# A decoder layer on one core: start offsets of the split weights, the layout of the KV weights, and elementwise work between GpSimd, VectorE and ScalarE

## Chip, core and metric

The kernel runs on one core of a Trainium2 chip. The metric is the device time of one execution in microseconds, here the median of three runs. The engines are TensorE (PE, with its weight loads PEld), VectorE (DVE), ScalarE (ACT), GpSimd (POOL) and SyncE (SP), which issues the DMAs.

## What is computed

One decoder layer in float32 on 256 tokens of width 2048: a mixer of two attentions, a cross-attention over 256 memory tokens, and an MLP of width 8192 with a squared ReLU, each followed by a layer norm of the scaled residual.

```python
def reference(x, mem, ...):
    h = x
    for l in range(DEPTH):                      # DEPTH = 1
        mix = hybrid_mixer(h, w_in[l], ...)
        h = layer_norm(DN_ALPHA * h + mix, ln1_g[l], ln1_b[l])
        xa = memory_cross_attention(h, mem, xa_w_q[l], xa_w_kv[l], xa_w_o[l])
        h = layer_norm(DN_ALPHA * h + xa, ln2_g[l], ln2_b[l])
        ff = squared_relu_mlp(h, mlp_w1[l], mlp_w2[l])
        h = layer_norm(DN_ALPHA * h + ff, ln3_g[l], ln3_b[l])
    return h

def hybrid_mixer(x, w_in, ...):
    h = x @ w_in                                # queries, keys, values, gates
    y_a = swa_sink_attention(...)               # sliding window of 128, 16 heads
    y_b = nsa_attention(...)                    # compressed, selected and window branch, 16 heads
    merged = sigmoid(g_a) * (y_a @ w_branch_swa) + sigmoid(g_b) * (y_b @ w_branch_nsa)
    return merged @ w_mix_out
```

## The kernel before

**Numbers.** Every float32 matrix product is made of three TensorE products of rounded parts. A weight chunk and an activation are each split into h, the value rounded to the matmul's 32-bit format, and l, the rest; the product is h·h + h·l + l·h.

**Chunks.** The weights come in chunks of 128 x 1024 float32 (512 KB; the first 16 are 1072 wide). SP loads a chunk into a tile `raw` (five buffers). `emit_splits` splits it: ScalarE casts it to h (line 198) and VectorE subtracts h from it to give l (line 199). h and l each have four buffers of 1152 columns, of which a chunk uses a part that begins at a start offset, `shift`, counted in columns of 4 bytes. `run_chunks` goes through all chunks in the program's order: it issues the loads, splits up to three chunks ahead (fewer for the first six, and one less for the chunks in `evac_first`), and issues the chunk's matmuls; `post` empties the PSUM banks at a block's end. Each engine executes its instructions in the order in which they were issued.

**Blocks.** A block is a run of chunks that fill the same PSUM banks.
- `make_c`, the KV block: 16 chunks with all keys, values and gates of the two attentions. Each makes six 432-column matmuls with the values' weights moving (`mm_x`, lines 231 to 238) and fifteen 256-column matmuls with the keys' weights stationary (`mm_w`, lines 246, 248, 249). `kv_parts` says how the raw columns go into h and l: keys first, the values behind from column 640 on, in three copies on each engine (four in the first chunk).
- `block_b`, 512 output columns with the weights stationary. For each 128 x 128 piece there is a pair: line 318 has h stationary and 512 moving columns (the activation's h and l), line 319 has l stationary and 256 moving columns. It is used for the queries of `w_in`, the keys and queries of the cross-attention, and `mlp_w1` from column 1024 on: 20 blocks of 8 chunks. Its offset goes round from chunk to chunk:

```python
shift=((0, 96, 48)[len(chunks) % 3],) * 2))
```

- `block_w`, the first 1024 columns of `mlp_w1`, with the weights stationary, 256 moving columns and the fixed offset (16, 112).
- `block_x`, the rest, with the weights moving in 512 columns and the offset 0; `mlp_w2` is the longest.

**Work beside the chunks.** `Side` holds jobs that run a piece at a time between chunks: the softmaxes (`softmax_job`), transposes and layer norms. In a softmax job VectorE adds the bias and takes the maximum, ScalarE takes the exponentials (line 734), VectorE the reciprocal of the sum, GpSimd multiplies the 512 columns by it (line 745), and TensorE transposes the result (line 749). There are 36 jobs; the 512 columns are two regions of 256 or four of 128. The compressed branch has four such multiplies on GpSimd (line 822). At the end of a `w_branch_nsa` block, `evac_bb` multiplies each PSUM bank by its gate on VectorE (line 955) and GpSimd adds it to `merged` (line 956); those banks are then taken by the next block. A layer norm's `norm_a` is a scale and shift on ScalarE (line 1037), a multiply on VectorE (line 1038) and an add on GpSimd (line 1039). `finish` does the last layer norm behind the row blocks of `mlp_w2` and ends with lines 1044 and 1048 on VectorE and the stores.

Of the kernel before, what the change touches and what calls it, by code (L numbers as in the profile page):

```python
# [12 lines left out]
F32R = mybir.dt.float32r  # L13
# [25 lines left out]
def fp(ap):  # L39
    return ap.bitcast(F32)  # L40


class Chunk:
    def __init__(self, loads, n, mm, pre=None, with_split=None, post=None, cap=AHEAD, extra=None, parts=None, shift=(0, 0)):
        self.loads, self.n, self.mm = loads, n, mm
        self.pre, self.with_split, self.post, self.cap = pre, with_split, post, cap
        self.extra, self.shift = extra, shift
        self.parts = parts or [((lambda r: r[:, :n]),) * 2]

# [61 lines left out]
def layer(ctx: ExitStack, tc: tile.TileContext, x, mem, w_in, attn_sinks, rel_bias_table,  # L111
# [77 lines left out]
    def emit_splits(upto):  # L189
        while state["split"] <= min(upto, len(chunks) - 1):  # L190
            c = state["split"]
            ch = chunks[c]
            if ch.extra:
                h, l = ch.extra()
            else:
                h, l = (split_tile(t)[:, c0:] for t, c0 in zip("hl", ch.shift))
            for src, dst in ch.parts:
                nc.scalar.copy(dst(h), src(raws[c]))  # L198
                nc.vector.tensor_sub(dst(l), src(raws[c]), fp(dst(h)))  # L199
            hs[c], ls[c] = h, l  # L200
            consumed.add(c)
            if ch.with_split:
                ch.with_split()
            state["split"] += 1

    def run_chunks():
        for i, ch in enumerate(chunks):
            if ch.pre:
                ch.pre()
            emit_loads()  # L210
            side.phase("ev")
            ahead = i + min(ch.cap, 1 if i < 3 else 2 if i < 6 else AHEAD)
            emit_splits(min(ahead, i + AHEAD - 1) if i in evac_first else ahead)
            emit_loads()
            ch.mm(hs[i], ls[i])
            if ch.post:
                ch.post()
                emit_splits(ahead)
                emit_loads()
            side.phase("pe")  # L220
# [85 lines left out]
    def block_b(w, n0, rhs, evac, tags=("acc",) * 4, pre=None):  # L306
# [3 lines left out]
        for k0 in range(0, KD, 2):  # L310
# [10 lines left out]
            def post():  # L321
# [4 lines left out]
            chunks.append(Chunk(loads, 1024, mm, pre=pre if k0 == 0 else None, post=post if k0 + 2 == KD else None,  # L326
                                shift=((0, 96, 48)[len(chunks) % 3],) * 2))

# [159 lines left out]
    def kv_loads(k):  # L488
# [8 lines left out]
        return own + more  # L497

    def kv_parts(k):
        def pairs(v0, v1):  # L500
            return (lambda r: r[:, 128:896].rearrange("p (b v n) -> p v b n", v=2, n=P)[:, v0:v1],
                    lambda r: r[:, 128:896].rearrange("p (v b n) -> p v b n", v=2, n=P)[:, v0:v1])

        def cols(c0, c1):
            return (lambda r: r[:, c0:c1],) * 2
        if k == 0:
            return [pairs(1, 2), cols(896, 1072), pairs(0, 1), cols(0, 128)]
        return [pairs(0, 2), cols(896, 1072), cols(0, 128)]

# [61 lines left out]
    def make_c():  # L571
        for k in range(KD):
            def mm(h, l, k=k):
# [4 lines left out]
                xh, xl = xk(k)  # L578
                first, last, V = k == 0, k == KD - 1, slice(640, 1072)
                rows = [slice(s * P, (s + 1) * P) for s in range(2)]  # L580
# [8 lines left out]
                else:  # L589
                    mm_x({(0, 0): a[0][:, :432], (1, 0): a[1][:, :432]},  # L590
                         lambda s: xh[:, rows[s]], lambda s: xl[:, rows[s]], h, l, [(640, 1072)], False, last)
                outs = [a[2][:, :S], cbox["c"][:, :S], cbox["c"][:, S:], a[2][:, S:], a[3][:, :S]]
                mm_w(outs, xh, xl, h, l, first, last, (0, 1, 4), (2, 3, 4), (0, 128, 512, 256, 384))

# [109 lines left out]
    def softmax_job(n, s, qk, regions, order, pv, gate=None, sink=None, first=False, stop=False, done=False, last=False):  # L704
# [36 lines left out]
        if gate is not None:  # L741
            smv = two(sm) if len(gate.shape) == 3 else sm
            nc.vector.tensor_mul(smv, smv, gate)
        pr = p.rearrange("p (r w) -> p r w", r=nr)
        nc.gpsimd.tensor_mul(pr, pr, sm.unsqueeze(2).to_broadcast([P, nr, 512 // nr]))  # L745
        yield "pe"
# [45 lines left out]
    def cmp_job(n):  # L792
# [28 lines left out]
        nc.vector.tensor_mul(cm[:, 1, 0:4], cm[:, 1, 0:4], rowmask.to_broadcast([P, 4]))  # L821
        nc.gpsimd.tensor_mul(pv, pv, cm[:, 1].unsqueeze(2).to_broadcast([P, 8, 32]))
        yield "pe"
# [125 lines left out]
    def evac_bb(n0):  # L949
        def evac(acc):  # L950
            m = merged()
            for (s, b), a in acc.items():
                c = n0 + 512 * b
                t = box["pb"].tile([P, 512], F32, tag="xp", name="gtmp", bufs=3)
                nc.vector.scalar_tensor_tensor(t, box["tb"][:, s, c:c + 512], 1.0, a, op0=OP.add, op1=OP.mult)
                nc.gpsimd.tensor_add(m[:, s, c:c + 512], m[:, s, c:c + 512], t)
            if n0 == 0:
# [75 lines left out]
    def norm_a(s, c0, w, add=None, mul=None):  # L1033
# [4 lines left out]
        (mul or nc.vector).tensor_mul(v, v, gb[:, 0, c0:c0 + w])  # L1038
        (add or nc.gpsimd).tensor_add(v, v, gb[:, 1, c0:c0 + w])

# [90 lines left out]
    def xa_job(h):  # L1131
# [33 lines left out]
        hilo(box["oth"][:, h, :], box["otl"][:, h, :], o[:, :S])  # L1165

    block_b(xa_w_kv[0], 0, me, evac_t("kt", None))
    evac_first.add(len(chunks) - 1)
    block_x(xa_w_kv[0], KD, 512, 256, me, evac_v(0))
# [9 lines left out]
    def after_wo(s, b):  # L1179
# [14 lines left out]
        norm_late(1, 256, 256)  # L1194
        norm_a(0, 256, 256, add=nc.vector)
        norm_shift(1)
# [13 lines left out]
    def between_wo(s, b):  # L1210
        if (s, b) == (1, 2):
            norm_shift(0)
            norm_a(0, 0, 256, mul=nc.gpsimd)

# [147 lines left out]
```

## Time and profile before

| | us |
|---|---|
| median of three runs (lowest, highest) | 1413.92 (1413.91, 1414.34) |
| the profiled execution's own time | 1414.3 |
| its span in the profile | 1412.3 |
| TensorE busy | 1394.8 |
| VectorE busy | 919.2 |
| ScalarE busy | 721.7 |
| GpSimd busy | 113.5 |

The span runs from the first to the last instruction of the profiled execution. A matmul's row has a start and a length; matmuls overlap in the array, so the step from one start to the next tells how long one takes in a row of them. The granted TensorE clock of the execution was 0.997 of full speed.

### The profile page before, as it was taken

Reading aid. Unit: us, or ns where it says so; the run is one execution under the profiler, and the core shown is the slowest. Engines: PE = TensorE matmul, PEld = TensorE weight load, DVE = VectorE, ACT = ScalarE, POOL = GpSimd, SP = SyncE. Lnnn points to the kernel's source line nnn. Section 1 sums busy time; section 2 is a strip of 40 time slices with the busy share of each in tenths; the row PEclk is TensorE's granted clock in tenths of the full one; section 3 lists DMA queues with packets and bytes.
Section 4 is the critical chain, followed back from the end, with each engine's and each line's share of the span. In section 5 each row is a group of like instructions: output and inputs, shape, how many; then the busy total and the mean of one; then the engine's idle time right before and its main releaser. Section 6 shows DMA issues by size and latency. Waiting matters only on the chain.

```text
span 1412.3 us, 20010 instructions
## 1 busy us (share of the span) xinstructions
PE 1394.8 (99%) x7458; PEld 1196.6 (85%) x7458; DVE 919.2 (65%) x1501; ACT 721.7 (51%) x1177; POOL 113.5 (8%) x111
## 2 busy tenths in 40 slices
PE   9999999999999999999999999999999999999996
PEld 8988888888888888898898888888888888888885
DVE  5677887677764756766955656556565555755566
ACT  5566676665664444455454444444454444444452
POOL 1000221111110400220320000000000000000002
PEclk9999999999999999999999999999999999999998
DMA  8786655555557585574466666666676666576662
GB/s 267 230 258 181 186 168 164 165 153 161 149 150 252 175 297 184 174 243 139 139 186 194 186 189 190 184 190 180 194 240 195 195 193 193 179 208 193 194 193 89
DMA packets 108529, 268.43 MB, mean 190 GB/s; under 512 B 9920, under 2 KB 24832, under 8 KB 107664
## 3 DMA queue, kind: packets, MB, share of 16 engines
q1 hardware_dynamic: 106096, 256.49, 59.9%
q0 software_dynamic: 2048, 10.54, 2.2%
q8 instruction: 58, 0.95, 0.3%
q14 instruction: 39, 0.32, 0.1%
q10 hardware_dynamic: 288, 0.13, 0.1%
HBM read 264.97 MB, written 2.15 MB: 189 GB/s over the span
## 4 chain that ended last, share of the span: by engine, by line
PE 67%; issue 26%; DVE 5%; ACT 1%; POOL 0%; DMA 0%; DVEq 0%; SPq 0%; ACTq 0%; POOLq 0%
PE acc L238 22%; PE acc L318 20%; PE acc L319 10%; DVE l L199 2%; PE acc L248 1%; PE acc L249 1%; PE acc L246 1%; PE acc L231 1%; PE acc L233 1%; PE acc L232 1%; PE pt L749 1%; PE o L758 1%; PE lg L715 1%; PE lg L714 1%; PE hid L610 1%
## 5 line engine op out<-in xcount | busy, mean ns | idle before, releaser
L199 DVE TENSOR_TENSOR l<-raw,h 128x1024 fp32r<-128x1024 f32 (+4 forms) x501 | 585.9, 1178 | 381.6 <-ACT h L198 377.6
L198 ACT CAST h<-raw 128x1024 fp32r<-128x1024 f32 (+4 forms) x501 | 493.4, 994 | 441.6 <-PE acc L238 205.7
L318 PE MATMUL acc<-h2t,h 128*128 128x512 f32 x896 | 314.7, 395 | 0.0
L319 PE MATMUL acc<-h2t,l 128*128 128x256 f32 x896 | 251.7, 281 | 0.0
L318 PEld LDWEIGHTS acc<-h2t,h 128*128 128x128 f32 x896 | 168.4, 188 | 40.0
L319 PEld LDWEIGHTS acc<-h2t,l 128*128 128x128 f32 x896 | 168.6, 188 | 0.0
L238 PE MATMUL acc<-h,xt 128*128 128x512 f32 (+1 forms) x504 | 149.8, 394 | 0.0
L238 PE MATMUL acc<-l,ah 128*128 128x512 f32 x476 | 146.6, 389 | 0.0
L238 PE MATMUL acc<-h,ah 128*128 128x512 f32 x476 | 146.5, 389 | 0.0
L238 PE MATMUL acc<-h,al 128*128 128x512 f32 x476 | 146.5, 389 | 0.0
L238 PEld LDWEIGHTS acc<-l,ah 128*128 128x128 f32 x476 | 89.3, 188 | 18.6
L238 PEld LDWEIGHTS acc<-h,al 128*128 128x128 f32 x476 | 89.3, 188 | 18.6
L238 PEld LDWEIGHTS acc<-h,ah 128*128 128x128 f32 x476 | 89.3, 188 | 18.5
L238 PEld LDWEIGHTS acc<-h,xt 128*128 128x128 f32 x504 | 91.1, 188 | 14.8
L318 PE MATMUL acc<-xt,h 128*128 128x512 f32 x256 | 91.4, 397 | 0.0
L238 PE MATMUL acc<-l,xt 128*128 128x512 f32 (+1 forms) x252 | 79.6, 388 | 0.0
L319 PE MATMUL acc<-xt,l 128*128 128x256 f32 x256 | 71.9, 281 | 0.0
L238 PE MATMUL acc<-h,mt 128*128 128x512 f32 x224 | 63.2, 394 | 0.0
L745 POOL TENSOR_TENSOR p<-p,st 128x512 f32<-128x512 f32 x36 | 39.1, 1086 | 297.5 <-DVE st L740 135.2
L734 ACT ACTIVATE p<-p,st 128x256 f32<-128x256 f32 (+1 forms) x96 | 42.7, 447 | 36.4 <-DVE st L729 36.4
L318 PEld LDWEIGHTS acc<-xt,h 128*128 128x128 f32 x256 | 48.1, 188 | 10.9 <-ACT gt L550 0.3
L238 PE MATMUL acc<-h,yt 128*128 128x512 f32 x192 | 55.5, 395 | 0.0
(298 smaller groups left out, 2025.7 us busy)
## 6 DMA issues: line engine op xcount, KB each, us to landing
raw<-in_mlp_w_dram SPq DMA_DIRECT2D x256, 512.0 KB, 4.5
raw<-in_w_in_dram SPq DMA_DIRECT2D x96, 512.0 KB, 3.6
raw<-in_w_mix_out_dram SPq DMA_DIRECT2D x32, 512.0 KB, 4.7
raw<-in_w_branch_swa_dram SPq DMA_DIRECT2D x16, 512.0 KB, 3.7
raw<-in_w_branch_nsa_dram SPq DMA_DIRECT2D x16, 512.0 KB, 4.6
raw<-in_xa_w_kv_dram SPq DMA_DIRECT2D x16, 512.0 KB, 4.3
raw<-in_w_in_dram SPq DMA_DIRECT2D x16, 408.0 KB, 4.7
tbias<-udram POOLq DMA_DIRECT2D x8, 512.0 KB, 5.2
```

The costliest lines, as they stand in the source:

```text
L198: nc.scalar.copy(dst(h), src(raws[c]))
L199: nc.vector.tensor_sub(dst(l), src(raws[c]), fp(dst(h)))
L231: nc.tensor.matmul(a, lhsT=xh(s), rhs=h[:, c0:c1], start=first, stop=False)
L232: nc.tensor.matmul(a, lhsT=xh(s), rhs=l[:, c0:c1], start=False, stop=False)
L233: nc.tensor.matmul(a, lhsT=xl(s), rhs=h[:, c0:c1], start=False, stop=last)
L238: nc.tensor.matmul(acc[s, b], lhsT=lhs(s), rhs=rhs[:, c0:c1], start=False, stop=False)
L246: nc.tensor.matmul(a, lhsT=h[:, c], rhs=xh, start=first and (t % 2 == 0 if opens is None else t in opens), stop=False)
L248: nc.tensor.matmul(a, lhsT=h[:, c], rhs=xl, start=False, stop=False)
L318: nc.tensor.matmul(o, lhsT=h[:, c], rhs=rhs.both(k), start=k == 0, stop=False)
L319: nc.tensor.matmul(o[:, :S], lhsT=l[:, c], rhs=rhs(k)[0], start=False, stop=k == KD - 1)
L734: nc.scalar.activation(p[:, c:c + w], p[:, c:c + w], AF.Exp, bias=nm[:, i:i + 1], accum_out=sm[:, i:i + 1])
L745: nc.gpsimd.tensor_mul(pr, pr, sm.unsqueeze(2).to_broadcast([P, nr, 512 // nr]))
```

## The change

It has five parts. (1) In `block_b` the start offset of h is always 16 columns (64 bytes) and that of l 112 columns (448 bytes). (2) In the KV chunks the values come first, and the keys stand behind them, h's from column 464 and l's from column 496 on; a part can now give h and l places of their own, and there are five copies per chunk on each engine. (3) The multiply of the softmax is done for each region by itself, on VectorE and ScalarE in turn; the multiply of the compressed branch goes to VectorE. (4) The add into `merged` and the adds of `norm_a` go from GpSimd to VectorE; one of `between_wo`, 256 wide, stays on GpSimd. (5) The first two key chunks of the cross-attention are split into a tile of their own, `kspare`, and a chunk's `boost` lets the splits run one or two chunks further ahead there.

```diff
@@ emit_splits
-            for src, dst in ch.parts:
-                nc.scalar.copy(dst(h), src(raws[c]))
-                nc.vector.tensor_sub(dst(l), src(raws[c]), fp(dst(h)))
+            for src, dst, *low in ch.parts:
+                h_ap = dst(h)
+                nc.scalar.copy(h_ap, src(raws[c]))
+                nc.vector.tensor_sub((low or [dst])[0](l), src(raws[c]), fp(h_ap))
@@ run_chunks
-            ahead = i + min(ch.cap, 1 if i < 3 else 2 if i < 6 else AHEAD)
+            ahead = i + ch.boost + min(ch.cap, 1 if i < 3 else 2 if i < 6 else AHEAD)
@@ block_b
-                                shift=((0, 96, 48)[len(chunks) % 3],) * 2))
+                                shift=(16, 112)))
@@ kv_parts
-        if k == 0:
-            return [pairs(1, 2), cols(896, 1072), pairs(0, 1), cols(0, 128)]
-        return [pairs(0, 2), cols(896, 1072), cols(0, 128)]
+        vals = [(lambda r: raw(r, 1, 2, 1), at(0, 2, True)), (lambda r: r[:, 896:1072], at(256, 176))]
+        ks = [(lambda r: r[:, 0:128], *keys(0, 128)), (lambda r: raw(r, 0, 3, 0), *keys(128, 3, True)),
+              (lambda r: raw(r, 0, 1, 1), *keys(512, 1, True))]
+        return vals + ks
@@ make_c
-                mm_w(outs, xh, xl, h, l, first, last, (0, 1, 4), (2, 3, 4), (0, 128, 512, 256, 384))
+                mm_w(outs, xh, xl, h[:, KEYS[0]:], l[:, KEYS[1]:], first, last, (0, 1, 4), (2, 3, 4), (0, 128, 512, 256, 384))
@@ softmax_job
-        pr = p.rearrange("p (r w) -> p r w", r=nr)
-        nc.gpsimd.tensor_mul(pr, pr, sm.unsqueeze(2).to_broadcast([P, nr, 512 // nr]))
+        for i, (c, w, h) in enumerate(regions):
+            if i % 2:
+                nc.scalar.mul(p[:, c:c + w], p[:, c:c + w], sm[:, i:i + 1])
+            else:
+                nc.vector.tensor_scalar(p[:, c:c + w], p[:, c:c + w], sm[:, i:i + 1], None, op0=OP.mult)
@@ the compressed branch
-        nc.gpsimd.tensor_mul(pv, pv, cm[:, 1].unsqueeze(2).to_broadcast([P, 8, 32]))
+        nc.vector.tensor_mul(pv, pv, cm[:, 1].unsqueeze(2).to_broadcast([P, 8, 32]))
@@ evac_bb
-                nc.gpsimd.tensor_add(m[:, s, c:c + 512], m[:, s, c:c + 512], t)
+                nc.vector.tensor_add(m[:, s, c:c + 512], m[:, s, c:c + 512], t)
@@ norm_a
-        (add or nc.gpsimd).tensor_add(v, v, gb[:, 1, c0:c0 + w])
+        (add or nc.vector).tensor_add(v, v, gb[:, 1, c0:c0 + w])
@@ the blocks of the cross-attention
+    def kspare(j):
+        if j == 0:
+            box["kspare"] = box["pb"].tile([P, 4, 1024], F32R, tag="memraw", name="kspare")
+        return box["kspare"][:, 2 * j], box["kspare"][:, 2 * j + 1]
+
+    c0 = len(chunks)
     block_b(xa_w_kv[0], 0, me, evac_t("kt", None))
+    for j in range(2):
+        chunks[c0 + j].extra = lambda j=j: kspare(j)
+    for i, b in enumerate((1, 2, 2, 1)):
+        chunks[c0 - 2 + i].boost = b
@@ between_wo
-            norm_a(0, 0, 256, mul=nc.gpsimd)
+            norm_a(0, 0, 256, add=nc.gpsimd, mul=nc.gpsimd)
```

The order of VectorE's instructions at the first merged evacuation, at the end of the first `w_branch_nsa` block (`gtmp` is the product that is added to `merged`, `acc` a PSUM bank, `tb` the gate). Before:

```order
L199 TENSOR_TENSOR l<-raw,h 128x1024 x12
L955 SCALAR_TENSOR_TENSOR gtmp<-tb,acc 128x512 x4
L199 TENSOR_TENSOR l<-raw,h 128x1024 x3
L385 TENSOR_TENSOR mt_4858<-tr,mt_4858 128x2x256
L199 TENSOR_TENSOR l<-raw,h 128x1024
```

After:

```order
L201 TENSOR_TENSOR l<-raw,h 128x1024 x12
L967 SCALAR_TENSOR_TENSOR gtmp<-tb,acc 128x512
L968 TENSOR_TENSOR merged<-merged,gtmp 128x512
L967 SCALAR_TENSOR_TENSOR gtmp<-tb,acc 128x512
L968 TENSOR_TENSOR merged<-merged,gtmp 128x512
L967 SCALAR_TENSOR_TENSOR gtmp<-tb,acc 128x512
L968 TENSOR_TENSOR merged<-merged,gtmp 128x512
L967 SCALAR_TENSOR_TENSOR gtmp<-tb,acc 128x512
L968 TENSOR_TENSOR merged<-merged,gtmp 128x512
L201 TENSOR_TENSOR l<-raw,h 128x1024 x3
```

The four evacuations of PSUM banks stood in a row and now have an add behind each.

VectorE at the tail, from the first row block's statistics on (`res` is the residual, `gb` the norm's scale and shift). Before:

```order
L1031 SCALAR_TENSOR_TENSOR rstd<-mv,rstd 128x1
L1038 TENSOR_TENSOR res<-res,gb_10109 128x512 x2
L1014 SCALAR_TENSOR_TENSOR res<-res,acc 128x512
L1020 BN_STATS stats<-res 128x6
L1038 TENSOR_TENSOR res<-res,gb_10109 128x512 x2
L1014 SCALAR_TENSOR_TENSOR res<-res,acc 128x512
L1020 BN_STATS stats<-res 128x6
L1026 BN_AGGR mv<-stats 128x2
```

After:

```order
L1043 SCALAR_TENSOR_TENSOR rstd<-mv,rstd 128x1
L1050 TENSOR_TENSOR res<-res,gb_10228 128x512
L1051 TENSOR_TENSOR res<-res,gb_10228 128x512
L1050 TENSOR_TENSOR res<-res,gb_10228 128x512
L1051 TENSOR_TENSOR res<-res,gb_10228 128x512
L1026 SCALAR_TENSOR_TENSOR res<-res,acc 128x512
L1032 BN_STATS stats<-res 128x6
L1050 TENSOR_TENSOR res<-res,gb_10228 128x512
L1051 TENSOR_TENSOR res<-res,gb_10228 128x512
L1050 TENSOR_TENSOR res<-res,gb_10228 128x512
L1051 TENSOR_TENSOR res<-res,gb_10228 128x512
L1026 SCALAR_TENSOR_TENSOR res<-res,acc 128x512
```

Two adds stand ahead of each of the last two evacuations (lines 1014 before, 1026 after).

ScalarE around the first key chunks of the cross-attention (`met` is the transposed memory, `h1t` the transposed result of the first layer norm). Before:

```order
L384 CAST met_5241<-tr 128x2x256
L198 CAST h<-raw 128x1024 x17
L1037 ACTIVATE res<-res,rstd 128x512
L198 CAST h<-raw 128x1024
L1037 ACTIVATE res<-res,rstd 128x512
L198 CAST h<-raw 128x1024 x3
L384 CAST h1t_5753<-ntr 128x4x128
```

After:

```order
L386 CAST met_5363<-tr 128x2x256
L200 CAST h<-raw 128x1024 x14
L200 CAST kspare<-raw 128x1024 x2
L200 CAST h<-raw 128x1024 x3
L1049 ACTIVATE res<-res,rstd 128x512
L200 CAST h<-raw 128x1024
L1049 ACTIVATE res<-res,rstd 128x512
L200 CAST h<-raw 128x1024
```

The first two key chunks are cast into `kspare`, and 19 casts instead of 17 stand ahead of the norm's first scale and shift.

## Rows read from the trace of the kernel before

**Rows 1.** The page: busy time, share of the span and instructions of each engine.

```profile
PE 1394.8 (99%) x7458; PEld 1196.6 (85%) x7458; DVE 919.2 (65%) x1501; ACT 721.7 (51%) x1177; POOL 113.5 (8%) x111
```

**Rows 2.** Window 770 to 1050, line 318: window, length, PE busy, PEld busy, clock, DMA.

```profile
770.00:1050.00 280.00, 280.00 (x798) 149.82 (x798) 1.00 0.65 193
```

**Rows 3.** Timeline of PE in `mlp_w1`, line 318: start, length, engine, line, operation.

```profile
840.80 0.40 PE L318 MATMUL acc<-h2t,h 128*128 128x512 f32 x1
...
843.59 0.40 PE L318 MATMUL acc<-h2t,h 128*128 128x512 f32 x1
...
843.94 0.40 PE L318 MATMUL acc<-h2t,h 128*128 128x512 f32 x1
...
844.30 0.40 PE L318 MATMUL acc<-h2t,h 128*128 128x512 f32 x1
...
846.77 0.39 PE L318 MATMUL acc<-h2t,h 128*128 128x512 f32 x1
```

**Rows 4.** Timeline of PE in `block_w`; then window 1090 to 1370, line 238.

```profile
718.27 0.28 PE L248 MATMUL acc<-h2t,h 128*128 128x256 f32 x1
...
720.19 0.28 PE L246 MATMUL acc<-h2t,h 128*128 128x256 f32 x1
...
1090.00:1370.00 280.00, 274.72 (x1213) 227.35 (x1212) 1.00 0.64 194
```

**Rows 5.** Timeline of PE in a KV chunk, first and last of 15 matmuls.

```profile
23.85 0.28 PE L246 MATMUL acc<-xt,h 128*128 128x256 f32 x1
...
25.52 0.28 PE L249 MATMUL acc<-xt,l 128*128 128x256 f32 x1
```

**Rows 6.** Timeline at LN1, all engines; in brackets the idle before, and its releaser.

```profile
587.40 1.30 POOL L1039 TENSOR_TENSOR res<-res,gb 128x512 f32<-128x512 f32 x1 [1.32 <-DVE res L1038]
...
587.56 2.21 DVE L199 TENSOR_TENSOR l<-raw,h 128x1024 fp32r<-128x1024 f32 x1 [0.25 <-ACT h L198]
...
589.83 0.39 PE L319 MATMUL acc<-met,l 128*128 128x256 f32 x1 [1.00 <-DVE l L199]
```

**Rows 7.** Timeline at LN2, all engines.

```profile
699.83 1.21 DVE L199 TENSOR_TENSOR l<-raw,h 128x1024 fp32r<-128x1024 f32 x1
...
700.05 2.12 POOL L1039 TENSOR_TENSOR res<-res,gb 128x512 f32<-128x512 f32 x1 [2.42 <-DVE res L1038]
...
702.23 0.55 PE L1055 MATMUL ntr<-ident,res 128*128 128x128 f32 x3 [0.89 <-POOL res L1039]
```

**Rows 8.** Lines 745 (with its waiters), 734, 1148; window 165 to 192, five engines.

```profile
L745 POOL TENSOR_TENSOR p<-p,st x36: 1036/1042/1451, 141.7 to 417.0; 128x512 f32<-128x512 f32 x36
...
  PEld pt L749: 3.4, 6
...
  PE pt L749: 1.0, 1
...
L734 ACT ACTIVATE p<-p,st x96: 384/448/512, 137.9 to 412.7; 128x256 f32<-128x256 f32 x48, 128x128 f32<-128x128 f32 x48
...
L1148 DVE TENSOR_SCALAR xp<-xp,xst x8: 346/351/355, 644.7 to 659.3; 128x256 f32<-128x256 f32 x8
...
165.00:192.00 27.00, 26.79 (x139) 21.96 (x138) 25.01 (x63) 21.72 (x49) 5.64 (x5) 1.00 0.55 158
```

**Rows 9.** Timeline at the first merged evacuation, VectorE and PE.

```profile
461.75 2.80 DVE L955 SCALAR_TENSOR_TENSOR gtmp<-tb,acc 128x512 f32<-128x512 f32 x4 [1.09 <-PE acc L233]
...
465.63 0.39 PE L231 MATMUL acc<-h,yt 128*128 128x512 f32 x1
```

**Rows 10.** Timeline of the tail, VectorE.

```profile
1396.07 1.40 DVE L1038 TENSOR_TENSOR res<-res,gb 128x512 f32<-128x512 f32 x2 [0.89 <-ACT res L1037]
...
1400.95 0.67 DVE L1014 SCALAR_TENSOR_TENSOR res<-res,acc 128x512 f32<-128x512 f32 x1
...
1402.76 3.15 DVE L1044 SCALAR_TENSOR_TENSOR res<-res,mv,gb 128x512 f32<-128x512 f32 x4
...
1405.90 2.85 DVE L1048 SCALAR_TENSOR_TENSOR res<-res,rstd,gb 128x512 f32<-128x512 f32 x5
```

More of the change, by code (lines that the diff above doesn't have):

```diff
@@ L47, in __init__ @@
         self.extra, self.shift = extra, shift
+        self.boost = 0
         self.parts = parts or [((lambda r: r[:, :n]),) * 2]
@@ L497, in kv_loads, with raw, at, ap @@
         return own + more
+    KEYS = (464, 496)
     def kv_parts(k):
[L500 to L505, printed above, removed]
-        if k == 0:
-            return [pairs(1, 2), cols(896, 1072), pairs(0, 1), cols(0, 128)]
-        return [pairs(0, 2), cols(896, 1072), cols(0, 128)]
+        def raw(r, b0, n, v):
+            return r[:, 128:896].rearrange("p (b v n) -> p b v n", v=2, n=P)[:, b0:b0 + n, v]
+        def at(c0, n, b=None):
+            def ap(t):
+                return t[:, c0:c0 + n * P].rearrange("p (b n) -> p b n", n=P) if b else t[:, c0:c0 + n]
+            return ap
+        def keys(c0, n, b=None):
+            return tuple(at(k0 + c0, n, b) for k0 in KEYS)
+        vals = [(lambda r: raw(r, 1, 2, 1), at(0, 2, True)), (lambda r: r[:, 896:1072], at(256, 176))]
+        ks = [(lambda r: r[:, 0:128], *keys(0, 128)), (lambda r: raw(r, 0, 3, 0), *keys(128, 3, True)),
+              (lambda r: raw(r, 0, 1, 1), *keys(512, 1, True))]
+        return vals + ks
     cbox = {}
@@ L578, in mm @@
                 xh, xl = xk(k)
-                first, last, V = k == 0, k == KD - 1, slice(640, 1072)
+                first, last, V = k == 0, k == KD - 1, slice(0, 432)
                 rows = [slice(s * P, (s + 1) * P) for s in range(2)]
@@ L590, in mm @@
                     mm_x({(0, 0): a[0][:, :432], (1, 0): a[1][:, :432]},
-                         lambda s: xh[:, rows[s]], lambda s: xl[:, rows[s]], h, l, [(640, 1072)], False, last)
+                         lambda s: xh[:, rows[s]], lambda s: xl[:, rows[s]], h, l, [(0, 432)], False, last)
                 outs = [a[2][:, :S], cbox["c"][:, :S], cbox["c"][:, S:], a[2][:, S:], a[3][:, :S]]
-                mm_w(outs, xh, xl, h, l, first, last, (0, 1, 4), (2, 3, 4), (0, 128, 512, 256, 384))
+                mm_w(outs, xh, xl, h[:, KEYS[0]:], l[:, KEYS[1]:], first, last, (0, 1, 4), (2, 3, 4), (0, 128, 512, 256, 384))
             def post():
@@ L1194, in after_wo @@
         norm_late(1, 256, 256)
-        norm_a(0, 256, 256, add=nc.vector)
+        norm_a(0, 256, 256)
         norm_shift(1)
```

## The prediction, as written before the changed kernel had run

> **What bounds the kernel now.** I read the page first, then the steps between matmul starts in single blocks, then the few places where TensorE waits. The page's first rows say that TensorE is busy for 99% of the span, VectorE for 65% and ScalarE for 51%; the row of TensorE is the one that matters [rows 1]. So a microsecond is won in two ways only: each matmul takes less time, or a wait of TensorE goes. The other engines count where TensorE waits for them, and in the tail after the last matmul.
>
> The step from matmul to matmul is not the same everywhere, and on that most of the forecast rests. A `block_b` pair is one 512-column matmul with h stationary and one 256-column matmul with l stationary. The program has 20 such blocks of 8 chunks with 8 pairs each: 1280 pairs, 896 of them in the MLP. Over 280 us of the MLP 798 pairs pass, 0.3509 us a pair [rows 2]. Within that, eight pairs take 2.79 us in one stretch (840.80 to 843.59) and 2.83 in the next (843.94 to 846.77), with single steps of 0.36 (843.94 to 844.30) [rows 3]. Operation, shapes and moving operand are the same in both, and the rows show no wait there. What goes round in threes, from chunk to chunk, is the start of h and l inside their tiles (0, 384, 192 bytes).
>
> Two other blocks show what the same matmuls cost elsewhere. The first MLP block (`block_w`) already has the offsets that the change gives to `block_b`, the same moving tile `h2t` and 256 columns: 17 steps from 718.27 to 720.19, 0.1129 us each. `mlp_w2` moves 512 columns of the weights: in the rows of line 238, 1213 matmuls in 274.72 us of busy time, 0.2265 each [rows 4]. The sum of the two, 0.340, is what I take for a pair that nothing disturbs.
>
> **The sum, part by part**, is made against the profiled execution: 1414.3 us, of which the span is 1412.3; the other 2.0 I leave as they are. The median of the three runs is 0.4 us lower, less than the 0.2% (2.8 us) that a measurement of this kernel can tell from no change.
>
> *Offsets in `block_b`.* h starts at 64 and l at 448 bytes, always, as in `block_w`. A pair loses 0.3509 - 0.340 = 0.0109 us. 16 of the 1280 belong to the two key chunks that go to a tile of their own and take neither offset: 1264 x 0.0109 = 13.8. I take -13.7. No row shows these offsets with 512 moving columns, so the term has bounds: 0 if the offset isn't the cause, and +11.5 if every pair gets the 0.36 [rows 3]. The value stands at the end of the `block_w` row [rows 4], which shares the weights' offsets, the order of loads of h and l, and the moving tile, and differs only in the moving length.
>
> *Keys behind values.* In the KV chunks the 256-column matmuls of the keys take 14 steps in 1.67 us, 0.1193 each [rows 5], against 0.1129 in `block_w` [rows 4]. The change gives h and l of the keys starts of their own (464 and 496 columns). 16 chunks x 15 matmuls x 0.0064 = 1.5; I take -1.4 (0 to -1.5). Five copies stand in place of three for the same columns, on ScalarE and on VectorE. Even if each of the two more cost a whole 256-column operation (0.35 on VectorE [rows 8]), that is 0.7 us in a chunk that holds 15 x 0.119 us of key matmuls and six of 432 columns (1.2 us), which covers it as long as VectorE keeps its third of idle time; uncovered it would be 16 x 0.7 = 11, and I see no sign of that. The first cast that TensorE waits for becomes 256 columns wide instead of 384: -0.1.
>
> *LN1 and the first key chunks.* At 587.56 a split's subtraction takes 2.21 us while GpSimd's add at 587.40 runs beside it [rows 6]; alone it takes 1.21 [rows 7]. l comes late, and TensorE sits idle for 1.00 us before 589.83 [rows 6]. The change moves these adds to VectorE and splits two chunks more ahead: -1.0 (0 to -1.0). An add there costs 0.70, as a multiply does with no GpSimd beside it [rows 10]; VectorE gets the time back in splits that no longer stretch. Next to be late would be the same subtraction, behind a mul and an add (1.4 us); two chunks more, of 2.8 us each, cover that.
>
> *LN2.* TensorE's transposes start at 702.23 after 0.89 us of idle, when GpSimd's add of 2.12 us is done. On VectorE it follows its multiply, ahead of the split at 699.83, and is done by about 700.6; that split comes 0.7 later [rows 7], which the chunks ahead cover: -0.9 (0 to -0.9).
>
> *Softmax normalisation.* 36 multiplies on GpSimd, 1.04 us each, become two shares side by side: VectorE scales half of the regions (0.35 for 256 columns, by the rows of the cross-attention's line 1148), ScalarE the other (0.45, by line 734). A job's chain gets some 0.5 us shorter. TensorE waited for the old multiply once for 1.0 us, and its weight loads, which reach it in part, for 3.4 in six places [rows 8]. But from 165 to 192 VectorE is busy for 25.01 of 27 us, with five of these multiplies on GpSimd [rows 8]; five times 0.35 brings it to 26.8. What it falls behind there the three chunks split ahead must cover. I take -1.0, between -2.0 (the six places too) and +2.0 (all of the 1.75 and a little more passes on to TensorE).
>
> *Merged adds.* At the end of a `w_branch_nsa` block VectorE empties four banks in 2.80 us while GpSimd adds beside it. Now an add of about 0.67 to 0.70 stands after each bank, so the fourth is free at 461.75 + 4 x 0.70 + 3 x 0.67 = 466.5. TensorE wants it at 465.63 [rows 9]: 0.9 late, twice, +1.7 (0.8 to 2.0). This is a price.
>
> *Tail.* VectorE takes four adds between the last row blocks. Before, its evacuation of the last bank begins at 1400.95. Now mul, add, mul, add (2.8), evacuation and statistics (1.4) and the same four again (2.8) start at 1396.07, hence 1403.0 at most and 1402.7 with no gaps: 1.8 later. The four operations of line 1044 took 3.15 beside GpSimd and take 2.8 without. So the last pass, at 1405.90, begins at about 1407.3 [rows 10]: +1.4 (1.0 to 1.8).
>
> Sum: -13.7 - 1.4 - 0.1 - 1.0 - 0.9 - 1.0 + 1.7 + 1.4 = -15.0, hence **1399.3 us**. The four multiplies of the compressed branch that go to VectorE too I cost at nothing (256 columns, 0.35 to 0.45 us each by [rows 8], in the softmax stretch and inside its bounds), and TensorE's and SP's orders don't change.
>
> **Rivals.**
>
> *The offsets do part of it.* Fixed offsets may give every pair what the better chunk shows now, 2.79/8 = 0.3488 [rows 3], or get half-way to the floor. The gain is then 1264 x 0.0021 = 2.7 to 6.8 us: 1406.2 to 1410.3. For it speaks that the pair alternates 512 with 256 columns, which no row shows at these starts; against it that both halves stand alone at their floor [rows 4].
>
> *VectorE becomes the bound.* The crowded softmax stretch costs +2.0 instead of -1.0, and the waits at LN1 and LN2 come back as waits for VectorE (+1.9): 1404.2. For it speak the 25.01 of 27 us [rows 8], against it that a split shrinks from 2.21 to 1.21 without GpSimd beside it [rows 6, 7].
>
> *The offsets do nothing.* Then the 2.79 and 2.83 have another cause that turns with the chunks, and -13.7 and -1.4 fall away: 1414.4, no change. The Trainium skill speaks for this: by its page "SBUF — State Buffer", section "SBUF: two separate sides", only the ports that VectorE and GpSimd share contend, and TensorE never waits for anyone, so that a start address would not matter to it. The trace disagrees as far as it goes, with 2.79 and 2.83 us for the same eight pairs [rows 3].
>
> *Slower: the fixed offsets lock onto the bad phase.* Now the start goes round and a bad one costs a third of the chunks; fixed, it would cost all. At 0.36 a pair [rows 3] it is 1264 x 0.0091 = +11.5 in place of -13.7: 1424.5. The other terms sum to -1.3, so this gives a slower kernel from 0.3509 + (2.8 + 1.3)/1264 = 0.3541 us a pair on. For it speaks that l is now always loaded beside 512 moving columns from the same start, against it `block_w` at 0.1129 [rows 4].
>
> **Chances.** Forecast (1395 to 1402) 0.68; part of the offsets' gain 0.13; VectorE the bound 0.08; nothing from the offsets 0.05; bad phase 0.06. The first three are faster by over 0.2%, 0.89 together, of which I give 0.02 to same, since the weak end of the partial gain is near it: faster 0.87, same 0.07, slower 0.06. The range runs from 1394 (the forecast with every bound at its good end and some waits more) to 1409, which takes in VectorE as the bound and most of the partial gain.
>
> **What would show it.** In the profile after: `block_b` pairs 0.340 us apart and without the round of threes, so 823 in place of 798 in 280 us; key matmuls of the KV chunks 0.113 apart; no idle of 0.9 us or more at the first key chunks and at LN2's transposes; no subtraction of a split over 1.5 us; TensorE waiting some 0.9 us after each merged evacuation; the last pass 1.4 us later after the last matmul. It is wrong if pairs stay at 0.349 or above, or if waits for VectorE stand in the softmax stretch.

## The result and the profile after

The changed kernel is slower: 1421.27 us (median, 1421.0 to 1421.31) against 1413.91; the ratio is 1.0051, 95% interval 1.0033 to 1.0068. The forecast was 1399.3, and its range ended at 1409. The span of the profiled execution is 1419.5 us, 7.2 more than before.

The page of the profile first: busy time and share of the span, as in [rows 1].

```profile
PE 1399.5 (99%) x7458; PEld 1199.8 (85%) x7458; DVE 935.7 (66%) x1610; ACT 740.6 (52%) x1256; POOL 25.0 (2%) x45
```

GpSimd has lost its work as planned, and TensorE is busy for 4.7 us more. The `block_b` pairs answer to [rows 2] and [rows 3]. First the window over line 320 (318 before):

```profile
770.00:1050.00 280.00, 280.00 (x794) 149.85 (x793) 1.00 0.64 188
```

Then TensorE's timeline (start, length, engine, line, operation):

```profile
842.20 0.40 PE L320 MATMUL acc<-h2t,h 128*128 128x512 f32 x1
842.43 0.28 PE L321 MATMUL acc<-h2t,l 128*128 128x256 f32 x1
842.55 0.40 PE L320 MATMUL acc<-h2t,h 128*128 128x512 f32 x1
...
845.02 0.40 PE L320 MATMUL acc<-h2t,h 128*128 128x512 f32 x1
```

794 pairs pass instead of 798 (forecast: 823). Eight pairs, 842.20 to 845.02, take 2.82 us, everywhere; the round of threes is gone, but the step is 0.353 and not 0.340.

TensorE's instructions stand in the same order in both kernels, so the start of one and the same matmul in the two traces shows where time is lost. Worked out from the two timelines (us):

```
matmul                                       before    after    later by
first block_b pair                            58.17    57.40      -0.77
last before the first softmax in the stretch 164.53   163.98      -0.55
a product of the softmax, end of the stretch 197.13   202.33      +5.20
transposes that waited for GpSimd            285.64   289.69      +4.05
first merged evacuation begins               464.73   468.83      +4.10
after the second merged evacuation           490.21   496.24      +6.03
the pair that waited at LN1                  589.83   594.70      +4.87
the transposes that waited at LN2            702.39   706.35      +3.96
first pair of the MLP                        736.86   740.80      +3.94
last pair of the MLP                        1051.12  1057.02      +5.90
last matmul                                 1400.18  1406.09      +5.91
last pass of the last layer norm (VectorE)  1405.90  1413.15      +7.25
```

So 5.75 us are lost in 33 us of softmax, 1.96 in the MLP's pairs, 1.9 at the two merged evacuations, and 1.3 in the tail; LN1 and LN2 give 1.2 and 0.9 back.

What TensorE waits for, over the whole span (line waited for, total, times, longest):

```profile
PE o L769 <- ACT pth L386: 2.4, 3, 1.5
PE o L770 <- DVE ptl L387: 1.9, 4, 0.7
PE warm L142 <- DVE rowmask L148: 0.9, 1, 0.9
PE acc L233 <- DVE gtmp L967: 0.7, 2, 0.4
```

Before, the list had LN1's and LN2's waits [rows 6, 7], that for line 745 [rows 8] and one at the first cast, at 6.21 us:

```profile
PE acc L584 <- ACT h L198: 1.0, 1, 1.0
```

The wait for `rowmask` was there before too. The other four are gone, and in their place TensorE waits for the two halves of the transposed probabilities, `pth` from ScalarE and `ptl` from VectorE, and for the merged evacuation. The softmax stretch, the window of [rows 8] (PE, PEld, DVE, ACT, POOL busy; clock; DMA):

```profile
165.00:192.00 27.00, 24.28 (x121) 19.48 (x120) 21.65 (x59) 19.01 (x46) 0.75 (x1) 1.00 0.46 137
```

VectorE was busy for 25.01 us of this window before and is for 21.65 now. It isn't fuller; it waits too. What ScalarE waits for from 165 to 200:

```profile
ACT p L755 <- DVE st L749: 7.3, 4, 2.0
ACT p L743 <- DVE st L738: 3.2, 4, 1.0
```

And VectorE in the same stretch:

```profile
DVE qs_b L693 <- ACT qs_b L692: 4.5, 4, 1.5
DVE ptl L387 <- ACT pth L386: 0.9, 1, 0.9
```

Line 755 is ScalarE's share of the new multiply. It waits for VectorE's reciprocal, line 749, four times and 7.3 us in all. Then VectorE waits for `qs_b`, a cast that stands behind that multiply in ScalarE's queue: 4.5 us. One place in order, ScalarE's timeline:

```profile
178.19 0.69 ACT L755 ACTIVATE p<-p,st 128x128 f32<-128x128 f32 x2 [1.64 <-DVE st L749]
178.91 0.58 ACT L779 COPY yl<-o 64x512 f32<-64x512 f32 x1
179.50 0.61 ACT L692 CAST qs_b<-qraw 64x512 fp32r<-64x512 f32 x1
180.14 1.05 ACT L200 CAST h<-raw 128x1024 fp32r<-128x1024 f32 x1
182.06 0.51 ACT L743 ACTIVATE p<-p,st 128x256 f32<-128x256 f32 x1 [0.87 <-DVE st L738]
```

and VectorE's and TensorE's end of it:

```profile
180.15 0.69 DVE L693 TENSOR_TENSOR qs_b<-qraw,qs_b 64x512 fp32r<-64x512 f32 x1 [1.53 <-ACT qs_b L692]
...
184.42 0.51 PE L769 MATMUL o<-pth,vs 128*128 128x512 f32 x1 [1.53 <-ACT pth L386]
185.50 0.50 PE L770 MATMUL o<-ptl,vs 128*128 128x512 f32 x1 [0.57 <-DVE ptl L387]
```

ScalarE stands still for 1.64 us before its multiply, the cast of `qs_b` comes after that, VectorE stands still for 1.53 before its part, and the next maximum, exponentials and `pth` are late in turn. The last two rows are the bill.

The merged evacuation (as [rows 9]) and the tail (as [rows 10]), VectorE and one row of TensorE:

```profile
465.85 0.69 DVE L967 SCALAR_TENSOR_TENSOR gtmp<-tb,acc 128x512 f32<-128x512 f32 x1 [1.09 <-PE acc L235]
466.58 0.69 DVE L968 TENSOR_TENSOR merged<-merged,gtmp 128x512 f32<-128x512 f32 x1
...
469.83 0.68 DVE L967 SCALAR_TENSOR_TENSOR gtmp<-tb,acc 128x512 f32<-128x512 f32 x1
...
470.57 0.51 PE L233 MATMUL acc<-h,yt 128*128 128x512 f32 x1 [0.36 <-DVE gtmp L967]
...
1408.62 0.68 DVE L1026 SCALAR_TENSOR_TENSOR res<-res,acc 128x512 f32<-128x512 f32 x1
...
1410.43 2.73 DVE L1056 SCALAR_TENSOR_TENSOR res<-res,mv,gb 128x512 f32<-128x512 f32 x4
...
1413.15 2.86 DVE L1060 SCALAR_TENSOR_TENSOR res<-res,rstd,gb 128x512 f32<-128x512 f32 x5
```

The fourth bank is emptied from 469.83 on, an add behind each of the three before it, and TensorE goes on at 470.57. In the tail the last evacuation starts 2.5 us after TensorE's last matmul (1406.09) instead of 0.8 (1400.95 against 1400.18).

### The profile page after: what moved, and what is told of

It is laid out like the page before. It is cut to its first block, busy times and chain, and to the rows that moved or that the text cites. A ratio compares the mean times of both kernels' runs of the same rounds, so it can differ in the third digit from the quotient of the medians.

```text
span 1419.5 us, 19997 instructions
## 1 busy us (share of the span) xinstructions
PE 1399.5 (99%) x7458; PEld 1199.8 (85%) x7458; DVE 935.7 (66%) x1610; ACT 740.6 (52%) x1256; POOL 25.0 (2%) x45
## 4 chain that ended last, share of the span: by engine, by line
PE 93%; DVE 4%; ACT 2%; issue 1%; DVEq 0%; POOL 0%; ACTq 0%
PE acc L240 45%; PE acc L320 21%; PE acc L321 11%; PE acc L250 2%; PE acc L251 2%; PE acc L248 2%; PE acc L233 1%; PE acc L235 1%; PE acc L234 1%; PE pt L761 1%; DVE l L201 1%; PE hid L619 1%; PE o L770 1%; PE ntr L1067 1%; PE lg L724 1%
## 5 line engine op out<-in xcount | busy, mean ns | idle before, releaser
L201 DVE TENSOR_TENSOR l<-raw,h 128x1024 fp32r<-128x1024 f32 (+4 forms) x530 | 574.4, 1097 | 381.4 <-ACT h L200 376.3
L240 PEld LDWEIGHTS acc<-l,xt 128*128 128x128 f32 x252 | 47.3, 188 | 9.5
L1289 DVE TENSOR_TENSOR al<-a,ah 128x256 fp32r<-128x256 f32 x128 | 53.4, 417 | 0.0
```

The costliest lines, as they stand in the source:

```text
L201: nc.vector.tensor_sub((low or [dst])[0](l), src(raws[c]), fp(h_ap))
L240: nc.tensor.matmul(acc[s, b], lhsT=lhs(s), rhs=rhs[:, c0:c1], start=False, stop=False)
L1289: nc.vector.tensor_sub(l, src, fp(h))
```

## The experiments

All changes are to the changed kernel (1421.27) unless the text says otherwise. Times are medians.

```
run                                             us       against the kernel before (95%)
e1  offsets of block_b go round again         1418.57    1.0033 (1.0021 to 1.0044)
e2  softmax multiply on GpSimd                1416.92    1.0020 (1.0011 to 1.0030)
e3  softmax multiply all on VectorE           1417.48    1.0025 (1.0014 to 1.0035)
e4  56 pairs of offsets in the MLP            1418.02    one run
e5  h at 64, l at 0 bytes                     1408.49    0.9963 (0.9951 to 0.9976)
e6  merged and last adds on GpSimd            1417.80    1.0027 (1.0016 to 1.0039)
e7  kernel before, h at 64, l at 0 bytes      1403.90    0.9929 (0.9915 to 0.9944)
e8  e2, e5 and e6 together                    1400.60    0.9907 (0.9892 to 0.9922)
e9  e8 with h at 448, l at 0 bytes            1398.22    0.9890 (0.9875 to 0.9905)
e10 e8 with h at 448, l at 256 bytes          1398.15    0.9890 (0.9875 to 0.9905)
e11 adds of LN1 and LN2 on GpSimd             1422.15    1.0060 (1.0043 to 1.0076)
```

The changed kernel's own ratio is 1.0051 (1.0033 to 1.0068). The intervals of e1, e3, e6 and e11 overlap with it, and those of e8 to e10 with each other; there the time alone doesn't decide, and the rows of the trace are read with it.

**e1: are the fixed offsets worse than those that go round?**

```diff
-                                shift=(16, 112)))
+                                shift=((0, 96, 48)[len(chunks) % 3],) * 2))
```

> The changed kernel with one edit undone: the start offset in block_b goes round again (0, 384, 192 bytes for h and l alike). Theory 'the fixed offsets sit in a worse phase': pairs go from 0.3526 back to 0.3509 us, 794 to 798 pairs in 280 us of the MLP, and the time falls by about 2.1 us to 1419.2. Rival 'the pair has no better step than this, the offset is only noise': pairs and time as in the changed kernel, 1421.3 within 0.5.

1418.57, 2.7 us less than the changed kernel, and the pairs are back: the window over line 320 has 799 in 280 us. The first theory holds: this part of the change costs 2 to 3 us by itself, 1.96 of them in the MLP's pairs.

```profile
770.00:1050.00 280.00, 280.00 (x799) 149.85 (x798) 1.00 0.65 190
```

**e2 and e3: what hurts in the softmax?**

e2:

```diff
-        for i, (c, w, h) in enumerate(regions):
-            if i % 2:
-                nc.scalar.mul(p[:, c:c + w], p[:, c:c + w], sm[:, i:i + 1])
-            else:
-                nc.vector.tensor_scalar(p[:, c:c + w], p[:, c:c + w], sm[:, i:i + 1], None, op0=OP.mult)
+        pr = p.rearrange("p (r w) -> p r w", r=nr)
+        nc.gpsimd.tensor_mul(pr, pr, sm.unsqueeze(2).to_broadcast([P, nr, 512 // nr]))
```

> The changed kernel with the softmax multiply back on GpSimd in one piece (the other parts stay). If the new waits between 165 and 197 us come from this part: TensorE's +5.2 us there goes, the wait for GpSimd at 285 us (0.8) and smaller ones (0.5) come back, time about 1417.4. Rival 'they come from another part, the five copies or the fixed offsets': the waits stay and the time is 1421 or more.

e3:

```diff
-            if i % 2:
-                nc.scalar.mul(p[:, c:c + w], p[:, c:c + w], sm[:, i:i + 1])
-            else:
-                nc.vector.tensor_scalar(p[:, c:c + w], p[:, c:c + w], sm[:, i:i + 1], None, op0=OP.mult)
+            nc.vector.tensor_scalar(p[:, c:c + w], p[:, c:c + w], sm[:, i:i + 1], None, op0=OP.mult)
```

> The changed kernel with all of the softmax multiply on VectorE and none on ScalarE. Theory 'hand-over': what hurts is that ScalarE's share waits in its queue for VectorE's reciprocal, with casts for TensorE behind it; without that share the +5.2 us between 165 and 197 falls to 2 or less, time 1417 to 1418.5, though VectorE has more to do. Rival 'VectorE is full there': it has 0.35 us per job more, and the waits grow to 6.5 us or more, time 1422.5 or above.

e2 takes 1416.92, 4.35 less, and TensorE waits for nothing from 160 to 200. e3 takes 1417.48, inside what the hand-over theory named and 5 us below what a full VectorE would have given. The rows that decide are e3's. TensorE's waits from 160 to 200:

```profile
PE o L767 <- DVE ptl L387: 1.5, 3, 0.7
PE o L766 <- ACT pth L386: 0.4, 1, 0.4
```

VectorE's waits from 165 to 200:

```profile
DVE ptl L387 <- ACT pth L386: 1.9, 2, 0.9
```

And the window of the stretch, columns as above:

```profile
165.00:192.00 27.00, 25.08 (x129) 20.34 (x128) 25.11 (x66) 20.14 (x45) 0.75 (x1) 1.00 0.49 153
```

With twice as much of the multiply on VectorE, its wait for `qs_b` (4.5 us) is gone, it is busy for 25.11 us of the 27, and TensorE's waits fall from 4.3 us (2.4 + 1.9) to 1.9. By the starts of the same matmuls the stretch loses 2.3 us in e3 where the changed kernel loses 5.75. What cost most of the time was ScalarE's share: it waits for VectorE with casts behind it in ScalarE's queue. The 1.9 that are left are what a full VectorE can explain at most. That ScalarE waits is not the cost by itself. From 165 to 200 it waits for VectorE for 10.5 us (7.3 + 3.2) in the changed kernel, and for long in e3 and in e2 too:

```profile
ACT p L743 <- DVE st L738: 9.2, 4, 2.7
...
ACT p L743 <- DVE st L738: 7.0, 5, 2.0
```

But they all stand ahead of the exponentials, and VectorE waits for no `qs_b` there. It matters where in the queue a wait stands.

**e4: which offsets are good?** In the MLP each two chunks take another pair of starts, 64 bytes apart.

```diff
+    def scan(c):
+        j = (c - scanned["c0"]) // 2
+        return 16 * (1 + j % 7), 16 * (j // 7)
-                                shift=(16, 112)))
+                                shift=scan(len(chunks)) if w is scanned.get("w") else (16, 112)))
```

> The changed kernel with other start offsets in the 14 MLP blocks of block_b: each two chunks have another pair of starts, h at one of seven and l at one of eight places 64 bytes apart, 56 combinations with 16 pairs each. Theory 'phase': the step of a pair depends on the combination, and some show 0.340 (the sum of the two blocks at their floor), some 0.36. Rival 'no floor for this alternation': all lie between 0.346 and 0.36. The time itself is a mean over them and tells little, between 1414 and 1428.

The mean of a pair in ns, worked out from the starts of its matmuls without the first two pairs of each combination. Starts are addresses modulo 512 bytes as the program places the tiles (offset 0 is 448 for h and 192 for l; the moving tile starts at 448):

```
l \ h      0     64    128    192    256    320    384
   0    353.2  346.4  346.6  346.6  353.3  346.4  346.7
  64    350.1  350.4  347.1  346.6  350.1  350.9  353.1
 128    352.9  353.6  353.6  351.8  352.9  353.6  353.5
 192    340.3  351.9  350.0  353.8  353.6  352.2  340.0
 256    353.3  346.4  346.7  346.7  353.3  346.4  346.7
 320    350.1  350.4  347.1  346.7  350.0  350.9  353.1
 384    352.8  353.6  353.7  351.8  352.8  353.6  353.9
 448    340.3  351.9  350.0  353.9  353.6  352.1  340.0
```

The changed kernel's pair of starts is (0, 128): 352.9, one of the bad ones. Only (0, 192), (0, 448), (384, 192) and (384, 448) reach the 340 on which the forecast was built. The rows of l repeat every 256 bytes; the columns of h don't (with l at 192, 340.3 for h at 0 and 353.6 at 256). Each combination was entered once, from its neighbour in this order, so the map may depend on the order too. Two stretches of the timeline, (0, 192) and (0, 128), with the same line, operation and shapes:

```profile
740.50 0.39 PE L326 MATMUL acc<-h2t,h 128*128 128x512 f32 x1
...
745.60 0.39 PE L326 MATMUL acc<-h2t,h 128*128 128x512 f32 x1
...
1015.61 0.40 PE L326 MATMUL acc<-h2t,h 128*128 128x512 f32 x1
...
1019.50 0.40 PE L326 MATMUL acc<-h2t,h 128*128 128x512 f32 x1
```

15 pairs in 5.10 us are 0.340 each, 11 pairs in 3.89 are 0.354. "Phase" holds, with one thing less than I wrote: no combination came near a mean of 0.36; 0.354 is the worst.

**e5 and e7: a good pair of starts over whole blocks.**

```diff
-                                shift=(16, 112)))
+                                shift=(16, 0)))
```

> The changed kernel with one number changed: the start offset of l in block_b is 0 bytes instead of 448; h stays at 64. In the scan this pair of starts showed 226 and 114 ns, 0.340 a pair, and the changed kernel's own showed 0.3529. Theory 'phase of the two starts': 823 instead of 794 pairs in 280 us of the MLP and 1264 x 0.0126 = 15.9 us less, 1405.4. Rival 'the scan's steps do not last over a whole block': a gain of under 8 us, 1413 or more.

e7 is the same line in the kernel before:

> The kernel before with one line changed: the rotating offset of block_b replaced by h at 64 and l at 0 bytes. Theory 'phase': 1280 x 0.0109 = 14.0 us less than before, 1400.1. Rival 'other waits take the place of the shorter steps': over 1404.

Both fall short in part: 1408.49 (12.8 less than the changed kernel, 15.9 expected) and 1403.90 (10.0 less than the kernel before, 14.0 expected). In the MLP all 896 pairs run at 0.340; e7's window over line 318 has 824 in 280 us:

```profile
745.00:1025.00 280.00, 280.00 (x824) 154.56 (x824) 1.00 0.64 193
```

The 384 pairs outside the MLP don't: their means are 346 to 350 ns in both. In e5's first block the trace shows how they get there:

```profile
56.81 0.39 PE L320 MATMUL acc<-xt,h 128*128 128x512 f32 x1
...
57.15 0.39 PE L320 MATMUL acc<-xt,h 128*128 128x512 f32 x1
...
57.49 0.39 PE L320 MATMUL acc<-xt,h 128*128 128x512 f32 x1
57.71 0.28 PE L321 MATMUL acc<-xt,l 128*128 128x256 f32 x1
58.02 0.50 PE L320 MATMUL acc<-xt,h 128*128 128x512 f32 x1
...
58.47 0.39 PE L320 MATMUL acc<-xt,h 128*128 128x512 f32 x1
...
58.82 0.40 PE L320 MATMUL acc<-xt,h 128*128 128x512 f32 x1
...
59.17 0.39 PE L320 MATMUL acc<-xt,h 128*128 128x512 f32 x1
```

The steps are 0.34 until a pause at 57.71 to 58.02; after it they are 0.35 with the same weights' starts, tiles and lines, and stay there (by the starts in ns, a cycle of 231, 117, 233, 119). In the fourth block, behind a later pause, they go on at 0.340 again. So the starts are not all: the same pair of starts has more than one steady rhythm, and after a pause it can go on in another. e5's miss of 3.1 us fits these 384 pairs at about 9 ns each, 3.4 if all of it reaches the end.

**e6: the two prices that the prediction named.**

```diff
-                nc.vector.tensor_add(m[:, s, c:c + 512], m[:, s, c:c + 512], t)
+                nc.gpsimd.tensor_add(m[:, s, c:c + 512], m[:, s, c:c + 512], t)
...
-                norm_a(0, c, 512)
+                norm_a(0, c, 512, add=nc.gpsimd)
                 store(0, c, 512)
```

> The changed kernel with two adds back on GpSimd: the add into merged (8) and the adds of the last layer norm (4). If they cost what the prediction said (1.7 and 1.4): 1418.2. Rival 'a chunk ahead covers the merged add, the tail is bound by the stores': 1420.5 or more.

1417.80: 3.5 less, where 3.1 was expected. The merged add and the tail cost what they were said to, though GpSimd slows VectorE beside it again, as this row of its tail shows (two multiplies, 1.38 in all in the changed kernel by its 0.68 to 0.69 each):

```profile
1402.51 2.32 DVE L1050 TENSOR_TENSOR res<-res,gb 128x512 f32<-128x512 f32 x2
```

**e8, e9, e10: the parts put together.** e8 has e2's, e5's and e6's edits.

> The changed kernel with h at 64 and l at 0 bytes, the softmax multiply back on GpSimd, and the adds into merged and of the last layer norm back on GpSimd; keys behind values, the two key chunks ahead and the other adds on VectorE stay. If the parts add up: 1421.3 - 15.9 - 4.4 - 3.1 = 1397.9. If the shorter pairs turn into waits for the splits: 1400 or more.

1400.60, 2.7 more than the sum. TensorE's one wait of 1 us is the old one for GpSimd's multiply, so I looked for the missing 2.7 in the pairs outside the MLP, as in e5. Two more pairs of starts tested that; e9's edit, which in e10 is (112, 64):

```diff
-                                shift=(16, 0)))
+                                shift=(112, 0)))
```

> The kernel of the run that had l at 0 bytes, the softmax multiply and the two adds back on GpSimd (1400.6), with h at 448 bytes instead of 64 (h's start is 384 modulo 512, l's 192). In that run 384 pairs outside the MLP stayed in a cycle of 350 ns, though the MLP's 896 ran at 340. In the scan this pair of starts reached 226 and 114 ns within three pairs after a worse combination. Theory 'with this pair of starts the floor is reached from any state': all blocks at 0.340, 3.4 us less, 1397.2. Rival 'the state on entry decides, whatever the starts': 1400.6 within 0.6.

> As the run with h at 448 and l at 0 bytes, but l at 256 bytes (start 448 modulo 512), the other combination that reached 0.340 in the scan from a worse one. Same theory and rival: 1397.2, or 1400.6 within 0.6.

1398.22 and 1398.15: 2.4 us less than e8, of 3.4 expected. In e10 four of the six blocks outside the MLP have means of 340.0 to 340.8, the other two of about 345 (worked out from the starts, without steps over 0.42 us). These starts bring most pairs back to the floor after a pause, where (0, 192) seldom does; "from any state" was too much: e9's first block stays at 350 behind the pause at which e10's goes back to 340. That the two times agree all the same shows that not every pair out there counts: e10 leads by 0.66 us at the last pair of that block (78.59 against 79.25) and by 0.08 at the first of the next. e10 beats both kernels: 15.7 us less than the one before, ratio 0.989.

**e11: what helps at LN1 and LN2?**

```diff
-        (add or nc.vector).tensor_add(v, v, gb[:, 1, c0:c0 + w])
+        (add or nc.gpsimd).tensor_add(v, v, gb[:, 1, c0:c0 + w])
...
-        norm_a(0, 256, 256)
+        norm_a(0, 256, 256, add=nc.vector)
...
-                norm_a(0, c, 512)
+                norm_a(0, c, 512, add=nc.vector)
```

> The changed kernel with the adds of the first two layer norms back on GpSimd (14), the tail's four stay on VectorE, the two key chunks ahead stay. If the adds alone were the gain at both norms: +1.9, 1423.2. If the two chunks ahead cover the first norm's wait by themselves: only the second norm's 0.9 comes back, 1422.2.

1422.15, 0.9 more: the second case. TensorE's waits have LN2's back and not LN1's:

```profile
PE ntr L1067 <- POOL res L1051: 0.8, 1, 0.8
```

So the two key chunks split ahead suffice to take LN1's wait away, and the add on VectorE takes LN2's.

## Why the prediction was wrong, step by step

- *What bounds the kernel*: right. All that was lost and won was lost and won on TensorE and in the tail.
- *Offsets, -13.7*: wrong; +1.96 in the MLP by the traces, 2.7 in all by e1. The step that failed is the choice of the value: `block_w` [rows 4] was taken as the nearest row because it shares the starts, the moving tile and the order of loads "and differs only in the moving length". With 512 and 256 columns in turn the same starts give 0.353 us (794 pairs in 280 us; 352.9 ns in e4), and other starts give 0.340. The order of loads differs too, which the prediction missed: `block_w` loads h twice and l once for each piece, `block_b` each of them once. This is TensorE in `block_w` before:

```profile
718.27 0.28 PE L248 MATMUL acc<-h2t,h 128*128 128x256 f32 x1
718.38 0.28 PE L249 MATMUL acc<-h2t,l 128*128 128x256 f32 x1
718.49 0.28 PE L246 MATMUL acc<-h2t,h 128*128 128x256 f32 x1
718.61 0.28 PE L248 MATMUL acc<-h2t,h 128*128 128x256 f32 x1
```

  Which of the two differences keeps `block_w` at its floor, no run shows. The floor itself held: the two rows add up to 0.3394, the prediction took 0.340, and the best starts run at 340.0 ns (e4, e5). So did the reading that the start makes a difference in [rows 3]: but from a difference between starts it doesn't follow which start is good, and the change's was not among those that the trace showed.
- *The rivals*: the fourth, "the fixed offsets lock onto the bad phase", is what happened, at 0.353 instead of its 0.36; that is below 0.3541, the point from which it was to make the kernel slower alone. It got 6 in 100. The third falls, and with it what the prediction drew from the Trainium skill's page "SBUF — State Buffer", section "SBUF: two separate sides": e4's rows differ by up to 0.014 us a pair with the starts, so a start address does matter to TensorE. The Trainium skill's sentence that TensorE never waits for anyone stands where one engine might wait for another; these steps go with the starts of TensorE's own operands, and the sentence can't be read as ruling that out.
- *Softmax, -1.0, bounds -2.0 to +2.0*: wrong; +5.75 in the stretch and -1.1 from there to the merged evacuation (the wait at 285 and smaller ones gone, as forecast), +4.35 in all by e2. The step that failed is "two shares side by side": the time of the operations was counted, and VectorE's busy share, but not what ScalarE's share waits for. It waits for VectorE's reciprocal, and what stands behind it in ScalarE's queue, casts that VectorE and TensorE need, waits too. The upper bound was VectorE's 1.75 us of extra work and a little more; it had no term for ScalarE's share waiting, 7.3 us in the stretch, with casts behind it. (ScalarE's 0.45 a share was a small misreading as well: the row of line 734 mixes 256 and 128 columns, 0.384 to 0.512 us.) The second rival named VectorE as the new bound; e3 shows that its work explains 1.9 of TensorE's 4.3 us at most.
- *Keys behind values, -1.4, and the first cast, -0.1*: half. The first `block_b` pair starts 0.77 earlier. The first matmul after the casts starts 0.39 earlier (6.21 before, 5.82 now), but two matmuls on only 0.03 are left of it (6.71 and 6.67), so most of the gain comes from the key matmuls: their step went from 0.1193 [rows 5] to 0.1166 and not to 0.113. This part has no run of its own.
- *LN1 -1.0, LN2 -0.9*: right (-1.2 and -0.9), and e11 says which edit did which: at LN1 the chunks ahead suffice even with the adds on GpSimd, while the prediction counted on both. The row taken for a subtraction that runs alone, 1.21 us in [rows 7], has GpSimd's add beside it from 700.05 on; the value holds all the same (1.22 us, the median of the subtractions with no multiply or add on GpSimd beside them, in both kernels), and none takes over 1.48 us in the changed kernel, as forecast.
- *Merged adds +1.7, tail +1.4*: right (+1.9 and +1.3; e6: 3.5 for both).
- *The chances*: 0.87 for faster rested on one term with 13.7 of the 15.0 us, whose good end was taken from a row of another shape. Had that term been left open between its bounds, as rows without these starts at these shapes leave it, no change and slower would have had far more than 13 in 100 between them.

What stays open: why the step goes with the operands' addresses. The runs show the dependence on both starts, its period of 256 bytes in l's, and more than one rhythm for the same starts. Whether the moving tile's own start (448 in all of them) shifts the map wasn't tried, nor the scan in another order.

## What to carry to other kernels

Where the same matmul shows different steps in one trace, the operands' start addresses are a knob worth several per mille, but its best place has to be measured for the block's own shapes and order of loads: here the setting at which one block ran at its floor was a bad one for another. One kernel that gives each stretch another setting measures such a map in a single run, and a setting must then be tried with the pauses of its block. Before a step goes to another engine, write down what it waits for there and what stands behind it in that queue; here a further hand-over between two engines that already pass work to and fro cost 4.4 us (e2), though both had idle time.

## What the runs showed of the hardware that I had not expected

- A pair of matmuls takes 340.0 to 353.9 ns as the two stationary tiles' start addresses change, with the same line, shapes and moving tile (e4).
- With the same starts, pairs run at 340 ns before a pause and at 350 after it, to the end of the block (e5's first), and some starts come back to 340 within three pairs in the scan, (384, 192) and (384, 448) among them.
- VectorE's busy time in a window of a crowded stretch fell (25.01 to 21.65 us of 27) when it was given more work, as it had come to wait for the engine that shared that work (4.5 us for `qs_b`; no such wait in e3, and 25.11 us busy).
